# A two-layer decoder trunk on one core: accumulator tiles of one PSUM bank instead of two

## The chip, the core and the metric

One core of one Trainium2 chip runs the whole program in one launch. The metric is device time in microseconds (us) of that core. Before the change the runs took 1087.12, 1088.2 and 1092.54 us, so the median is 1088.2 us.

Engines are named as in the profile: PE is TensorE's matmul, PEld its weight load, DVE VectorE, ACT ScalarE, POOL GpSimd, SP SyncE, which here issues the weight DMAs. PSUM is the memory that matmuls write; the kernel allots it in banks of 128 partitions x 512 float32.

## The reference

Two layers over 256 positions of width 1024. Each layer is three residual steps on `x`:

```python
def swiglu(x, w_gate, w_up, w_down):
    return (jax.nn.silu(x @ w_gate) * (x @ w_up)) @ w_down
# per layer:
#   x = x + 0.5 * swiglu(rmsnorm(x, g0), ...)          first FFN, D_FF = 2816
#   x = x + concat(nsa_group(...), hgrn2(...)) @ w_out mix, fed by rmsnorm(x, g1) @ w_in
#   x = x + 0.5 * swiglu(rmsnorm(x, g2), ...)          second FFN
```

`nsa_group` is sparse attention (8 query heads, 2 key/value groups, compressed, selected and windowed keys, with norm and rotary on q and k), `hgrn2` is a gated linear recurrence with 4 heads. Everything is float32, and the weights of the two layers are read once.

## The kernel before

**The number format.** Each float32 weight tile is loaded by SP into a `raw` buffer (three of them, 512 KB each), rounded by ACT into `hi` (128x1024) and completed by DVE, or sometimes POOL, into `lo` = raw - hi. A ring of five hi/lo pairs feeds PE. Activations are split in the same way: `xx` holds the normalised, transposed input as high and low parts, `th`/`tl` the hidden layer of an FFN, `ah`/`al` the attention output. A product is three matmuls: hi x high, lo x high, hi x low.

**Two kinds of product.** `stream` (L462 and on, lines L486 to L488) keeps 128 positions of the activations stationary and moves 512 columns of weights; it runs once for each half `h` of the 256 positions. It serves the first FFN block, the `down` product and most of the mix. `wide_unit` (L501 and on) keeps 128 columns of weights stationary and moves all 256 positions. For the gate and up columns of the FFNs, paired blocks, it needs two matmuls: L519 moves the 512 columns "high | low" of `xx` against `hi`, L520 the 256 high ones against `lo`. Each block has 256 gate or up columns, that is two accumulators of one bank (index `c`), and an FFN has ten gate and ten up blocks. Lines L525 to L527 are the unpaired form in the mix.

**The accumulators.** PSUM has eight banks. `short` has three tiles and `po` one, for transposes and attention. The four others are two tiles, `acc0` and `acc1`, of two banks each; what the planner hands out as slots are the halves `t[:, i]` of these tiles. Gate blocks take both halves of `acc0`, up blocks both of `acc1`; a `stream` product of position half h takes one half of `acc{h}`.

**What follows a product.** Gate: ACT copies the right half of each bank into `sg` (both banks in one instruction, 128x512), DVE adds the left half, then the slots are released and ACT applies silu. Up: the same copy and add, then DVE multiplies with `sg`, ACT and DVE split the result into `th` and `tl`. In the mix, ACT and DVE read q, k, v and gates out of `acc` (names `buf`, `vv`, `xn`, `G`), and after each residual product DVE adds `acc` to `x` (L682).

**What sets the order.** The kernel is written as many small generators, which wait for keys (`wait`, `put`), take slots (`acq`, `rel`) and yield operations. The class `Sched` plans ahead of the run: it keeps an estimated end time for each engine and for each slot, gives each ready operation the time at which it could start plus a penalty (tables `PEN`, `STEP`, `PREP`, `FLOW`, `BIAS`, `SWITCH`, `FIRST`), and emits the smallest next. Each engine then runs its instructions in the emitted order. The waits between engines are not written by hand: they follow from which tile an instruction reads or writes, and `acc0` as a whole is one tile. Helpers record nearly all operations, so L335 is any ACT operation, L348 and L351 any two-operand one on DVE or POOL, L383 a transpose on PE.

Of the kernel before, what the change touches and what calls it, by code (L numbers as in the profile page):

```python
# [55 lines left out]

PEN = {"norm_turn": -0.1, "next_gain": 0.77, "gates_task": 0.15, "compress_task": -0.03, "level_task": 0.34, "boot":
       -1.1, "first_gain": -2.01, "first_norm": 0.02, "pad": 3.68, "hi_task": -0.6, "load_stream": 3.08, "done":
       -0.32, "kv_task": 1.05, "turn": -1.16, "load_w1": 2.22, "mix_prepare": 0.32, "c_turn": -1.52, "f_task": 0.04,
       "q_turn": 0.17, "kw_task": -4.22, "q_task": 0.59, "hg_task": 0.84, "hq_task": 0.54, "last_product": -0.25,  # L60
       "k_turn": 0.01, "products": -0.03, "turn_task": -0.1, "attend_task": 0.04, "out_task": 0.25, "k_task": 0.45,
       "cmp_task": -0.04, "first_turn": -0.43, "head_task": -0.08, "log_task": 0.04}
STEP = {'h': -0.47, 'g': 0.03, 'r': -0.0}
PREP = (-0.23, 0.26, 0.5, 0.92)
FLOW = (0.08, 0.28, 0.1)
BIAS = {'POOL': 0.14, 'ACT': -0.5}
SWITCH = 0.8

# [38 lines left out]
class Task:  # L107
    def __init__(self, gen, pen, deps, phase):
        self.gen, self.pen, self.deps, self.phase = gen, pen, list(deps), phase
        self.req = None  # L110

    def advance(self, value=None):
# [10 lines left out]
class Sched:  # L123
# [85 lines left out]
    def run(self):  # L209
        while self.tasks:  # L210
# [38 lines left out]
            self.free[eng] = issued if eng == "DMA" else end  # L249
            t.deps = [(end, eng)]  # L250
            self.advance(t, (end, eng))

# [50 lines left out]
class Trunk(Sched):  # L303
    def __init__(self, ctx, tc, io, out):
# [154 lines left out]
    def stream(self, h):  # L459
        for p, (a, b) in enumerate(self.phases):  # L460
            self.phase_at[h] = p
            for i in range(a, b):  # L462
# [27 lines left out]
                for t in range(2):  # L490
                    if i < BOOT:
                        yield wait(("lo", i, t))
                    yield self.P(3 * (WEIGHTS + k.n / 2400), lambda: mm(t))
                self.used[i] = self.used.get(i, 0) + 1
# [7 lines left out]
    def wide_unit(self, i, u, p):  # L502
# [35 lines left out]
        if u.last:  # L538
            self.spawn(k.done(k.ps[0]), phase=p, deps=self.keys[("wide", i)])
# [27 lines left out]
    def start(self):  # L567
        nc, per = self.nc, self.per
        self.X, self.XN, self.ss, self.rs = [], [], [], []
        self.XX = per.tile([128, 8, 2, 256], F32R, name="xx")  # L570
        self.XH, self.XL = self.XX[:, :, 0], self.XX[:, :, 1]
        for h in range(2):
# [6 lines left out]
        self.con = per.tile([128, C_END], F32, name="con")  # L579
        self.half = per.tile([128, 16], F32, name="half")  # L580
        self.grow, self.gcol = per.tile([8, 128], F32, name="grow"), per.tile([128, 8], F32, name="gcol")
# [139 lines left out]
    def ffn(self, l, pre):  # L721
# [27 lines left out]

        def both_parts(x, a):  # L750

            x, t = x.rearrange("p (c t) -> p c t", c=2), self.pair[a]
            yield self.A(x, t[:, :, 256:])
            yield self.tt(x, t[:, :, :256], x, OP.add)

        def wide_gate_done(b):
            def done(ps):
                yield wait(("open", p))
                (sg,) = yield acq("sg")
                yield from both_parts(sg, 0)  # L760
                yield rel("acc0", *ps)
                yield self.A(sg, sg, AF.Silu)
                st["wg", b] = sg
                yield put(("wg", p, b))
            return done

        def wide_up_done(b):
            def done(ps):
                (up,) = yield acq("sg")
                yield from both_parts(up, 1)  # L770
                yield rel("acc1", *ps)
                yield wait(("wg", p, b))
                sg = st["wg", b]
                yield self.tt(sg, up, sg, OP.mult)
                yield rel("sg", up)
                s = slice(2 + 2 * b, 4 + 2 * b)
                yield from self.split(st["th"][:, s], st["tl"][:, s], sg.rearrange("p (c t) -> p c t", c=2))
                yield rel("sg", sg)
                for h in range(2):
                    yield put(("h", p, h, 1 + b))  # L780
            return done
# [96 lines left out]
    def mix(self, l):  # L878
# [24 lines left out]
        def q_task(h, ps):  # L903
# [12 lines left out]
            for o, i in swap:  # L916
                a_.append((yield tt(t2[:, :, o], src[:, :, i], self.sg[:, h, 0:1, o].to_broadcast([128, H, 32]), OP.mult)))
            yield ("deps", a_)
            yield rel(f"acc{h}", ps)
# [648 lines left out]
```

## Time and profile before

| | before |
|---|---|
| runs | 1087.12, 1088.2, 1092.54 us |
| profiled execution | 1091.2 us, of which span 1089.4 us |
| PE busy | 1061.6 us, 97% of the span |
| DVE, ACT, POOL busy | 64%, 57%, 13% |
| DMA | 186 MB, mean 171 GB/s |

The profiled execution has 1.8 us around its span and is 3.0 us above the median of the runs. The stages of a layer follow each other: first FFN (to about 208 us in layer 0), mix (208 to 370 us), second FFN (to about 555 us); layer 1 repeats them. PE counts as busy from a matmul's start to a modelled end, so consecutive matmuls overlap in the record: the time that a matmul really takes from its neighbours is the distance from one start to the next.

### The profile page before, as it was taken

Reading aid. Unit: us, or ns where it says so; the run is one execution under the profiler, and the core shown is the slowest. Engines: PE = TensorE matmul, PEld = TensorE weight load, DVE = VectorE, ACT = ScalarE, POOL = GpSimd, SP = SyncE. Lnnn points to the kernel's source line nnn. Section 1 sums busy time; section 2 is a strip of 40 time slices with the busy share of each in tenths; the row PEclk is TensorE's granted clock in tenths of the full one; section 3 lists DMA queues with packets and bytes.
Section 4 is the critical chain, followed back from the end, with each engine's and each line's share of the span. In section 5 each row is a group of like instructions: output and inputs, shape, how many; then the busy total and the mean of one; then the engine's idle time right before and its main releaser. Section 6 shows DMA issues by size and latency. Waiting matters only on the chain.

```text
span 1089.4 us, 16298 instructions
## 1 busy us (share of the span) xinstructions
PE 1061.6 (97%) x6188; PEld 893.8 (82%) x6188; DVE 697.5 (64%) x1168; ACT 624.0 (57%) x1012; POOL 143.5 (13%) x111
## 2 busy tenths in 40 slices
PE   7999999999999999999999999999999989999998
PEld 4888888888787788888888888887978878888886
DVE  5776664668985666665366666448699666565633
ACT  6555554468884555564355555435789645555532
POOL 1000010211000012210031212002100001122110
PEclk9999999999999999999999999999999999999999
DMA  6766566556332566667566656656562326656653
GB/s 216 217 197 188 190 207 189 156 158 189 104 117 78 156 180 187 193 177 224 180 176 185 210 177 196 210 155 168 164 194 79 97 88 183 191 176 194 194 176 114
DMA packets 154159, 186.00 MB, mean 171 GB/s; under 512 B 7568, under 2 KB 117984, under 8 KB 154080
## 3 DMA queue, kind: packets, MB, share of 16 engines
q1 hardware_dynamic: 154080, 184.96, 56.5%
q8 instruction: 48, 0.79, 0.3%
q14 instruction: 31, 0.25, 0.1%
HBM read 183.89 MB, written 1.05 MB: 170 GB/s over the span
## 4 chain that ended last, share of the span: by engine, by line
PE 88%; DVE 5%; ACT 4%; issue 1%; DMA 1%; SPq 1%; POOL 0%; DVEq 0%; ACTq 0%; POOLq 0%
PE acc L519 27%; PE acc L520 14%; PE acc L486 12%; PE acc L487 12%; PE acc L488 12%; PE short L383 3%; PE po L1163 2%; ACT buf L335 1%; PE short L1381 1%; DVE lo L348 1%; PE acc L525 1%; PE acc L527 1%; PE acc L526 1%; ACT hi L335 1%; SPq L373 1%
## 5 line engine op out<-in xcount | busy, mean ns | idle before, releaser
L348 DVE TENSOR_TENSOR lo<-raw,hi 128x1024 fp32r<-128x1024 f32 (+2 forms) x300 | 356.4, 1202 | 177.0 <-ACT hi L335 176.6
L519 PE MATMUL acc<-xx,hi 128*128 128x512 f32 x1280 | 451.5, 397 | 0.0
L335 ACT ACTIVATE hi<-raw 128x1024 fp32r<-128x1024 f32 (+2 forms) x338 | 346.4, 1039 | 142.4 <-PE acc L488 83.2
L520 PE MATMUL acc<-xx,lo 128*128 128x256 f32 x1280 | 359.2, 281 | 0.0
L519 PEld LDWEIGHTS acc<-xx,hi 128*128 128x128 f32 x1280 | 240.3, 188 | 57.7
L520 PEld LDWEIGHTS acc<-xx,lo 128*128 128x128 f32 x1280 | 241.9, 189 | 0.2
L351 POOL TENSOR_TENSOR lo<-raw,hi 128x1024 fp32r<-128x1024 f32 x39 | 98.2, 2519 | 407.6 <-ACT hi L335 382.1
L486 PE MATMUL acc<-hi,th 128*128 128x512 f32 x352 | 140.0, 398 | 0.0
L488 PE MATMUL acc<-hi,tl 128*128 128x512 f32 x352 | 139.2, 396 | 0.0
L487 PE MATMUL acc<-lo,th 128*128 128x512 f32 x352 | 139.2, 395 | 0.0
L486 PE MATMUL acc<-hi,xx 128*128 128x512 f32 (+1 forms) x240 | 97.2, 405 | 8.0 <-DVE x L682 3.6
L348 DVE TENSOR_TENSOR sg<-acc,sg 128x512 f32<-128x512 f32 (+1 forms) x86 | 57.8, 672 | 54.9 <-ACT sg L335 54.7
L487 PE MATMUL acc<-lo,xx 128*128 128x512 f32 (+1 forms) x240 | 91.1, 380 | 0.2 <-DVE lo L348 0.2
L335 ACT ACTIVATE sg<-acc 128x512 f32<-128x512 f32 (+1 forms) x86 | 50.0, 581 | 71.3 <-PE acc L520 63.7
L488 PE MATMUL acc<-hi,xx 128*128 128x512 f32 (+1 forms) x240 | 90.8, 378 | 0.0
L488 PEld LDWEIGHTS acc<-hi,tl 128*128 128x128 f32 x352 | 66.2, 188 | 15.9
L486 PEld LDWEIGHTS acc<-hi,th 128*128 128x128 f32 x352 | 66.2, 188 | 15.7
L487 PEld LDWEIGHTS acc<-lo,th 128*128 128x128 f32 x352 | 66.2, 188 | 15.4
L335 ACT ACTIVATE th<-sg 128x512 fp32r<-128x512 f32 x40 | 25.3, 634 | 75.5 <-DVE sg L348 75.5
L486 PEld LDWEIGHTS acc<-hi,xx 128*128 128x128 f32 x240 | 45.1, 188 | 19.6 <-DVE x L682 5.3
L348 DVE TENSOR_TENSOR sg<-sg,sg 128x512 f32<-128x512 f32 x40 | 52.3, 1308 | 1.4
L488 PEld LDWEIGHTS acc<-hi,xx 128*128 128x128 f32 x240 | 45.1, 188 | 8.7
(211 smaller groups left out, 1149.8 us busy)
## 6 DMA issues: line engine op xcount, KB each, us to landing
raw<-in_ffn_w_down_dram SPq DMA_DIRECT2D x88, 512.0 KB, 4.3
raw<-in_ffn_w_gate_dram SPq DMA_DIRECT2D x80, 512.0 KB, 4.1
raw<-in_ffn_w_up_dram SPq DMA_DIRECT2D x80, 512.0 KB, 3.8
raw<-in_w_in_dram SPq DMA_DIRECT2D x48, 512.0 KB, 3.9
raw<-in_w_out_dram SPq DMA_DIRECT2D x16, 512.0 KB, 3.7
buf<-in_cmp_w_dram SPq DMA_DIRECT2D x16, 256.0 KB, 5.6
raw<-in_ffn_w_gate_dram SPq DMA_DIRECT2D x13, 256.0 KB, 2.8
raw<-in_ffn_w_up_dram SPq DMA_DIRECT2D x13, 256.0 KB, 3.1
```

The costliest lines, as they stand in the source:

```text
L335: return ("ACT", c, lambda: self.nc.scalar.activation(out, in_, func, **k), TABLES.get(func), False)
L348: alts = [("DVE", 0.065 + 0.00104 * n, lambda: self.nc.vector.tensor_tensor(out, a, b, op), None, not in_psum(a) and not in_psum(b))]
L351: alts.append(("POOL", 0.13 + 0.00213 * n, lambda: self.nc.gpsimd.tensor_tensor(out, a, b, op), None, True))
L373: return Op(("DMA", nbytes / 360e3, lambda: self.nc.sync.dma_start(out, in_), None, False))
L383: self.nc.tensor.transpose(o, i, self.ident[:i.shape[0], :i.shape[0]])
L486: f(ps[:, :k.n], ah, hi[:, t, :k.n], start=st, stop=False)
L487: f(ps[:, :k.n], ah, lo[:, t, :k.n], start=False, stop=False)
L488: f(ps[:, :k.n], al, hi[:, t, :k.n], start=False, stop=sp)
L519: f(self.pair[k.wide][:, c], hi[:, t, j], x, start=u.first and t == 0, stop=False)
L520: f(self.pair[k.wide][:, c, :256], lo[:, t, j], x[:, :256], start=False, stop=u.last and t == 3)
L525: f(ps[:, c], hi[:, t, j], xh, start=u.first and c == t == 0, stop=False)
L1163: nc.tensor.matmul(po[:, 64 * k:64 * k + 64], th[:, 128 * k:128 * k + 128], vv[:, vi, g], start=(i == k == 0), stop=False)
```

## The change

Four things are changed together.

1. The accumulators are four tiles of one bank, `acc00`, `acc01`, `acc10`, `acc11`, with two slots of `acc0` and two of `acc1` as before.
2. A gate or up block ends per bank: as soon as the matmuls of one index `c` of its last unit are emitted, its own evacuation starts, in operations of 128x256 instead of 128x512. The `sg` pool has eight tiles of 256 columns instead of five of 512. Key `("half", p, b)` makes the `down` product wait for both halves of a block.
3. `xx` is laid out with the two parts apart, [part, k, position] instead of [k, part, position]. For one k the high and low positions were 512 consecutive numbers of a partition; now they are two runs of 256, 8 KB apart, and the moving operand of L519 (L517 after) is that pair of runs.
4. The planner: a slot is free when the last operation of every engine of its task is over, not of the last operation alone; a 512-column product whose activations are not `xx` is priced 0.0065 us higher; the tables have new numbers. With these the emitted order changes.

```diff
-        self.pair = []
         for h in range(2):
-            t = psum.tile([128, 2, 512], F32, name=f"acc{h}")
-            self.pair.append(t)
-            self.slots[f"acc{h}"] = [(t[:, i], []) for i in range(2)]
+            self.slots[f"acc{h}"] = [(bank(f"acc{h}{i}"), []) for i in range(2)]
...
-            x = self.XX[:, u.kt + t].rearrange("p a t -> p (a t)")
-            f(self.pair[k.wide][:, c], hi[:, t, j], x, start=u.first and t == 0, stop=False)
-            f(self.pair[k.wide][:, c, :256], lo[:, t, j], x[:, :256], start=False, stop=u.last and t == 3)
+            f(ps[c].rearrange("p (a t) -> p a t", a=2), hi[:, t, j], self.XX[:, :, u.kt + t], start=u.first and t == 0, stop=False)
+            f(ps[c][:, :256], lo[:, t, j], self.XH[:, u.kt + t], start=False, stop=u.last and t == 3)
...
-                yield self.P(0.707 if k.paired else 6 * (WEIGHTS + 256 / 2400), lambda: two(c, t))
+                done = yield self.P(0.707 if k.paired else 6 * (WEIGHTS + 256 / 2400), lambda: two(c, t))
+            if k.paired and u.last:
+                self.spawn(k.done(c, k.ps[0][c]), phase=p, deps=[done])
...
-        self.XX = per.tile([128, 8, 2, 256], F32R, name="xx")
-        self.XH, self.XL = self.XX[:, :, 0], self.XX[:, :, 1]
+        self.XX = per.tile([128, 2, 8, 256], F32R, name="xx")
+        self.XH, self.XL = self.XX[:, 0], self.XX[:, 1]
...
-        def both_parts(x, a):
+        def both_parts(x, ps):
-            x, t = x.rearrange("p (c t) -> p c t", c=2), self.pair[a]
-            yield self.A(x, t[:, :, 256:])
-            yield self.tt(x, t[:, :, :256], x, OP.add)
+            yield self.A(x, ps[:, 256:])
+            yield self.tt(x, ps[:, :256], x, OP.add)
...
-                self.slots[arg].append((x, list(t.deps)))
+                self.slots[arg].append((x, list(t.deps) + [d for d in t.last.values() if d not in t.deps]))
...
-            self.slots["sg"] = [(pool.tile([128, 512], F32, name=f"sg{i}"), []) for i in range(5)]
+            self.slots["sg"] = [(pool.tile([128, 256], F32, name=f"sg{i}"), []) for i in range(8)]
...
-FIRST = (-0.31, -0.01, 0.65, 0.74, 1.09, 0.54, -1.08, 0.72)
+FIRST = (-0.15, -0.01, 0.61, 0.68, 1.4, 0.59, -1.31, 0.93)
```

The orders below show what this moves. The number behind a name tells tiles apart; a wait is shown with the engine whose work is waited for. In the changed kernel the three lines of `stream` are L485 to L487, the transposes L382, ACT's helper L334.

PE before, early in the mix of layer 0, where the products of q and k/v for the second half of the positions both stand in tile `acc1`:

```order
L486 MATMUL acc1_64<-hi0_72,xx_82 128x512
L487 MATMUL acc1_64<-lo0_73,xx_82 128x512
L488 MATMUL acc1_64<-hi0_72,xx_82 128x512
L486 MATMUL acc1_64<-hi0_72,xx_82 128x512 [waits Activation_49]
L487 MATMUL acc1_64<-lo0_73,xx_82 128x512
L488 MATMUL acc1_64<-hi0_72,xx_82 128x512
L486 MATMUL acc0_63<-hi1_74,xx_82 128x512 [waits DVE_49]
```

And PE after at the same place, with q in `acc11` and k/v in `acc10`:

```order
L485 MATMUL acc11_66<-hi3_80,xx_84 128x512
L486 MATMUL acc11_66<-lo3_81,xx_84 128x512
L487 MATMUL acc11_66<-hi3_80,xx_84 128x512
L485 MATMUL acc10_65<-hi0_74,xx_84 128x512
L486 MATMUL acc10_65<-lo0_75,xx_84 128x512
L487 MATMUL acc10_65<-hi0_74,xx_84 128x512
L485 MATMUL acc10_65<-hi0_74,xx_84 128x512
L486 MATMUL acc10_65<-lo0_75,xx_84 128x512
L487 MATMUL acc10_65<-hi0_74,xx_84 128x512
L485 MATMUL acc00_63<-hi1_76,xx_84 128x512 [waits Activation_49]
```

The wait for ACT between the two groups on `acc1` is gone; the one that is left after is on the ring's `hi1`. The order of the products themselves is the same.

PE before, at the end of the mix in layer 0, where the output product's second column block follows the first in tile `acc1`:

```order
L486 MATMUL acc1_64<-hi3_78,xx_82 128x512
L487 MATMUL acc1_64<-lo3_79,xx_82 128x512
L488 MATMUL acc1_64<-hi3_78,xx_82 128x512
L486 MATMUL acc1_64<-hi0_72,xx_82 128x512 [waits DVE_49]
L487 MATMUL acc1_64<-lo0_73,xx_82 128x512
L488 MATMUL acc1_64<-hi0_72,xx_82 128x512
L383 MATMUL short2_67<-ident_91,xn0_84 128x128 x4
L486 MATMUL acc1_64<-hi0_72,xx_82 128x512
```

And PE after at the same place:

```order
L485 MATMUL acc10_65<-hi3_80,xx_84 128x512
L486 MATMUL acc10_65<-lo3_81,xx_84 128x512
L487 MATMUL acc10_65<-hi3_80,xx_84 128x512
L485 MATMUL acc11_66<-hi0_74,xx_84 128x512
L486 MATMUL acc11_66<-lo0_75,xx_84 128x512
L487 MATMUL acc11_66<-hi0_74,xx_84 128x512
L382 MATMUL short2_69<-ident_93,xn0_86 128x128 [waits DVE_49]
L382 MATMUL short2_69<-ident_93,xn0_86 128x128 x3
L485 MATMUL acc11_66<-hi0_74,xx_84 128x512
```

The wait for DVE ahead of the second block is gone; a wait for DVE now stands ahead of the transposes of `xn0`, three matmuls later.

ACT before, in the first FFN of layer 0, around one gate and one up block:

```order
L335 ACTIVATE sg3_122<-acc1_64 128x512 [waits PE_49]
L335 ACTIVATE hi0_72<-raw2_71 128x1024 [waits DMAHW0_49,Activation_49]
L335 ACTIVATE th_124<-sg1_120 128x512 [waits DVE_49]
L335 ACTIVATE hi1_74<-raw0_69 128x1024 [waits DMAHW1_49,PE_49,Activation_49]
L335 ACTIVATE sg2_121<-acc0_63 128x512 [waits PE_49]
L335 ACTIVATE sg2_121<-sg2_121 128x512 [waits DVE_49]
```

And ACT after:

```order
L334 ACTIVATE sg0_121<-acc11_66 128x256 [waits PE_49]
L334 ACTIVATE hi3_80<-raw2_73 128x1024 [waits DMAHW2_49,Activation_49]
L334 ACTIVATE th_129<-sg6_127 128x256 [waits DVE_49]
L334 ACTIVATE sg2_123<-acc10_65 128x256 [waits PE_49]
L334 ACTIVATE th_129<-sg7_128 128x256 [waits DVE_49]
L334 ACTIVATE hi0_74<-raw0_71 128x1024 [waits DMAHW3_49,Pool_49]
L334 ACTIVATE sg4_125<-acc01_64 128x256 [waits PE_49]
L334 ACTIVATE sg4_125<-sg4_125 128x256 [waits DVE_49]
L334 ACTIVATE sg5_126<-acc00_63 128x256 [waits PE_49]
L334 ACTIVATE sg5_126<-sg5_126 128x256 [waits DVE_49]
```

Each operation on 512 columns has become two on 256. In the whole program 160 such operations of ACT and 160 of DVE become 320 each, and POOL takes 9 of the `lo` operations instead of 39; the 30 others stand on DVE.

## Rows read from the trace of the kernel before

**Rows 1.** Page, part 4: the chain that ended last, shares by engine

```profile
PE 88%; DVE 5%; ACT 4%; issue 1%; DMA 1%; SPq 1%; POOL 0%; DVEq 0%; ACTq 0%; POOLq 0%
```

**Rows 2.** Windows by stage: stretch, length, busy us (instructions) by engine, clock, DMA

```profile
26.00:145.00 119.00, 119.00 (x673) 102.70 (x672) 81.02 (x94) 68.65 (x88) 0.00 (x0) 1.00 0.64 197
208.00:370.00 162.00, 154.32 (x1161) 130.68 (x1160) 125.87 (x340) 115.19 (x254) 15.26 (x22) 1.00 0.46 132
370.00:490.00 120.00, 119.89 (x673) 103.42 (x672) 77.42 (x77) 66.00 (x85) 21.90 (x10) 1.00 0.64 188
742.00:904.00 162.00, 154.06 (x1159) 130.42 (x1158) 125.52 (x340) 115.93 (x254) 15.11 (x21) 1.00 0.45 131
```

**Rows 3.** Waits of PE: line, waited for, us in total, times, longest

```profile
PE acc L486 <- DVE x L682: 3.6, 4, 1.0
...
PE acc L486 <- ACT buf L335: 2.1, 4, 0.7
PE acc L486 <- ACT G L335: 1.4, 2, 0.7
...
PE acc L486 <- ACT xn L335: 1.1, 2, 0.7
PE acc L486 <- DVE buf L348: 1.0, 2, 0.5
```

**Rows 4.** Timeline of PE at 219 us: start, duration, instruction, idle before

```profile
219.34 0.39 PE L488 MATMUL acc<-hi,xx 128*128 128x512 f32 x1
220.42 0.50 PE L486 MATMUL acc<-hi,xx 128*128 128x512 f32 x1 [0.69 <-ACT buf L335]
220.76 0.39 PE L487 MATMUL acc<-lo,xx 128*128 128x512 f32 x1
```

**Rows 5.** Timeline of ACT at the same time

```profile
219.77 0.60 ACT L335 ACTIVATE buf<-acc 128x512 f32<-128x512 f32 x1 [0.70 <-PE acc L488]
```

**Rows 6.** Chain from 330 to 372 us: start, duration, piece

```profile
341.65 1.03 POOL ost L377
...
343.45 0.49 PE po L1432 x2
...
359.91 0.69 DVE x L682
360.65 0.50 PE acc L486
```

**Rows 7.** Window in the middle of layer 0's mix, columns as in rows 2

```profile
280.00:300.00 20.00, 19.81 (x213) 16.41 (x212) 18.60 (x85) 18.44 (x64) 1.06 (x2) 1.00 0.28 80
```

**Rows 8.** Instructions by form, ACT and DVE: count, busy us, mean ns, idle before

```profile
L335 ACT ACTIVATE sg<-acc 128x512 f32<-128x512 f32 x80 | 47.7, 596 | 64.2 <-PE acc L520 63.7
...
L335 ACT ACTIVATE sg<-acc 128x256 f32<-128x256 f32 x6 | 2.3, 386 | 7.1 <-PE acc L488 7.1
...
L348 DVE TENSOR_TENSOR lo<-raw,hi 128x1024 fp32r<-128x1024 f32 x286 | 346.3, 1225 | 171.3 <-ACT hi L335 171.0
L348 DVE TENSOR_TENSOR sg<-acc,sg 128x512 f32<-128x512 f32 x80 | 55.3, 691 | 53.3 <-ACT sg L335 53.0
...
L348 DVE TENSOR_TENSOR sg<-acc,sg 128x256 f32<-128x256 f32 x6 | 2.5, 419 | 1.7 <-ACT sg L335 1.7
```

**Rows 9.** Page, part 5: the two matmuls of a gate or up pair

```profile
L519 PE MATMUL acc<-xx,hi 128*128 128x512 f32 x1280 | 451.5, 397 | 0.0
...
L520 PE MATMUL acc<-xx,lo 128*128 128x256 f32 x1280 | 359.2, 281 | 0.0
```

**Rows 10.** Windows of line L519 alone, second FFN of layer 0, first of layer 1

```profile
400.00:480.00 80.00, 80.00 (x228) 42.59 (x227) 1.00 0.64 190
580.00:660.00 80.00, 80.00 (x232) 43.13 (x231) 1.00 0.64 190
```

**Rows 11.** Chain at 215 us: products with `xx` stationary, columns as in rows 6

```profile
214.97 0.23 PE acc L486
...
218.15 0.23 PE acc L488
```

More of the change, by code (lines that the diff above doesn't have):

```diff
@@ L55 @@
 ORDER = ('q', 'kv', 'kw', 'hf', 'hq', 'hi', 'hg')
[L57 to L62, printed above, removed]
+PEN = {"norm_turn": -0.1, "next_gain": 0.34, "gates_task": 0.15, "compress_task": -0.03, "level_task": 0.35, "boot":
+       -1.55, "first_gain": -3.16, "first_norm": 0.01, "pad": 4.23, "hi_task": -0.74, "load_stream": 3.09, "done":
+       -0.32, "kv_task": 1.24, "turn": -3.97, "load_w1": 2.22, "mix_prepare": 0.46, "c_turn": -0.45, "f_task": 0.13,
+       "q_turn": 0.17, "kw_task": -2.2, "q_task": 0.55, "hg_task": 0.78, "hq_task": 0.52, "last_product": -0.25,
+       "k_turn": 0.01, "products": -0.03, "turn_task": -0.1, "attend_task": 0.04, "out_task": 0.27, "k_task": 0.45,
+       "cmp_task": -0.01, "first_turn": -0.44, "head_task": -0.08, "log_task": 0.1}
 STEP = {'h': -0.47, 'g': 0.03, 'r': -0.0}
[L64 to L67, printed above, removed]
+PREP = (-0.22, 0.28, 0.5, 0.92)
+FLOW = (0.11, 0.29, 0.54)
+BIAS = {'POOL': 0.13, 'ACT': -0.5}
+SWITCH = 0.79
 def constants():
@@ L110, in __init__ @@
         self.req = None
+        self.last = {}
     def advance(self, value=None):
@@ L249, in run @@
             self.free[eng] = issued if eng == "DMA" else end
-            t.deps = [(end, eng)]
-            self.advance(t, (end, eng))
+            token = (end, eng)
+            t.deps, t.last[eng] = [token], token
+            self.advance(t, token)
 def four(t):
@@ L492, in stream @@
                         yield wait(("lo", i, t))
-                    yield self.P(3 * (WEIGHTS + k.n / 2400), lambda: mm(t))
+                    yield self.P(3 * (WEIGHTS + k.n / 2400 + 0.0065 * (k.n == 512 and u.act != self.xact)), lambda: mm(t))
                 self.used[i] = self.used.get(i, 0) + 1
@@ L534, in wide_unit @@
             for t in (0, 2):
-                yield self.P(0.707 if k.paired else 6 * (WEIGHTS + 256 / 2400), lambda: two(c, t))
+                done = yield self.P(0.707 if k.paired else 6 * (WEIGHTS + 256 / 2400), lambda: two(c, t))
+            if k.paired and u.last:
+                self.spawn(k.done(c, k.ps[0][c]), phase=p, deps=[done])
         yield rel("ring", self.split_w.pop(i))
         yield put(("wide", i))
-        if u.last:
+        if u.last and not k.paired:
             self.spawn(k.done(k.ps[0]), phase=p, deps=self.keys[("wide", i)])
@@ L579, in start @@
         self.con = per.tile([128, C_END], F32, name="con")
-        self.half = per.tile([128, 16], F32, name="half")
+        self.half = per.tile([128, 8], F32, name="half")
         self.grow, self.gcol = per.tile([8, 128], F32, name="grow"), per.tile([128, 8], F32, name="gcol")
@@ L748, in both_done, with done @@
             yield rel("short", pt)
-        def both_parts(x, a):
-            x, t = x.rearrange("p (c t) -> p c t", c=2), self.pair[a]
-            yield self.A(x, t[:, :, 256:])
-            yield self.tt(x, t[:, :, :256], x, OP.add)
+        def both_parts(x, ps):
+            yield self.A(x, ps[:, 256:])
+            yield self.tt(x, ps[:, :256], x, OP.add)
         def wide_gate_done(b):
-            def done(ps):
+            def done(c, ps):
                 yield wait(("open", p))
                 (sg,) = yield acq("sg")
-                yield from both_parts(sg, 0)
-                yield rel("acc0", *ps)
+                yield from both_parts(sg, ps)
+                yield rel("acc0", ps)
                 yield self.A(sg, sg, AF.Silu)
-                st["wg", b] = sg
-                yield put(("wg", p, b))
+                st["wg", b, c] = sg
+                yield put(("wg", p, b, c))
             return done
         def wide_up_done(b):
-            def done(ps):
+            def done(c, ps):
                 (up,) = yield acq("sg")
[L770 to L773, printed above, removed]
+                yield from both_parts(up, ps)
+                yield rel("acc1", ps)
+                yield wait(("wg", p, b, c))
+                sg = st["wg", b, c]
                 yield self.tt(sg, up, sg, OP.mult)
                 yield rel("sg", up)
-                s = slice(2 + 2 * b, 4 + 2 * b)
-                yield from self.split(st["th"][:, s], st["tl"][:, s], sg.rearrange("p (c t) -> p c t", c=2))
+                s = 2 + 2 * b + c
+                yield from self.split(st["th"][:, s], st["tl"][:, s], sg)
                 yield rel("sg", sg)
-                for h in range(2):
-                    yield put(("h", p, h, 1 + b))
+                if ("half", p, b) in self.keys:
+                    yield wait(("half", p, b))
+                    for h in range(2):
+                        yield put(("h", p, h, 1 + b))
+                else:
+                    yield put(("half", p, b))
             return done
```

2 lines of the change are left out of this document (1 added, 1 removed).

## The prediction, made before the changed kernel ran

> **What bounds the kernel now.** I read the chain of waits first. PE holds 88% of it, DVE and ACT together 9% [rows 1]: the time is the matmuls, plus what PE waits for. The windows by stage say where it waits. In an FFN PE is busy for all of a stretch, 119.00 of 119 us, while DVE is busy for 81.02 and ACT for 68.65 [rows 2]; in the mix of layer 0 PE is busy 154.32 of 162 us, so 7.7 us idle, and layer 1's mix is taken as the same. What is to be gained without fewer matmuls lies in those idle times. The list of PE's waits names them [rows 3]. Five of its lines have one thing in common, found by following each wait in the order back to the two addresses: the matmul that waits writes one bank of `acc0` or `acc1`, and the ACT or DVE operation waited for reads the other bank of the same tile. No data pass between them. The timeline shows one such case: ACT reads `acc` from 219.77 to 220.37 [rows 5], and PE starts its next matmul at 220.42 although the last one began at 219.34 [rows 4]. These five lines sum to 3.6 + 2.1 + 1.4 + 1.1 + 1.0 = 9.2 us in 14 waits.
>
> **Part 1, one-bank tiles.** It removes these waits wholly: in the order before each is there, in the order after no matmul on an accumulator waits for a reader of another bank. What one costs is more than the idle time shown, since busy time has a modelled end. With `xx` stationary a matmul takes 227 ns from start to start (214.97 to 218.15 us are 14 of them) [rows 11]. The case shown lost 220.42 - 219.34 - 0.23 = 0.85 us, 0.16 more than the 0.69 printed, and the first matmul after it took 220.76 - 220.42 = 0.34 instead of 0.23 us, 0.11 more [rows 4]. So 14 x 0.27 = 3.8 us on top of 9.2, 13.0 us in all.
>
> How much of it stays? The waits for `x` and `G` (5.0 us, 6 waits, so 6.6 us with the additions) stand at the end of the mix and lead into the FFN, where PE never waits; this part stays. One doubt is the output norm before it, ACT to DVE to POOL `ost` to PE `po` at 341.65 to 343.45 us [rows 6]: the few steps ahead of it go through a ring buffer that PE frees, so it comes earlier with PE. The waits for `buf` and `xn` (4.2 us, 8 waits, 6.4 us) stand early in the mix. Behind them PE runs into a stretch where DVE is busy 18.60 and ACT 18.44 of 20 us [rows 7]; if these two set the pace, PE arrives earlier and waits there. I keep half, 3.2 us. Sum: 6.6 + 3.2 = 9.8 us, with 6.6 and 13.0 as ends.
>
> **Part 2, evacuation per bank.** 160 operations of ACT on 512 columns become 320 on 256: 2 x 386 - 596 = 176 ns more each, 28 us; on DVE 2 x 419 - 691 = 147 ns, 24 us [rows 8], the accumulator reads standing for the silu, multiply and split of the same size. 30 `lo` operations move from POOL to DVE, at 1.225 us each [rows 8] 37 us. Over four FFNs that is 7 us on ACT and 15 on DVE for each. In the window 26 to 145 us they had 50 and 38 us idle [rows 2], so PE's own matmuls hide all of it, and I cost it at nothing. If the cover were gone, as in a stretch where DVE runs at 93%, up to 61 us could show; no accumulator is evacuated by these operations there. The gain of starting one bank's evacuation 4 pairs earlier is nothing either, since no FFN window has PE idle by over 0.11 us [rows 2]. The Trainium skill ("Advanced Engine Details and Errata", section The Read-Write Bubble) speaks against this part: ACT and DVE pay a latency between instructions, so tiles should be large, of 512 or 1024 elements. Its mechanism is in the trace, as the 176 and 147 ns above; taken as a verdict on the time it would give 1078 + 52, and the row of 119.00 busy us of 119 says that it doesn't reach PE.
>
> **Part 3, the layout of `xx`.** The stationary loads of `xx` stay contiguous. The 512-column matmul of 1280 pairs [rows 9] now reads two runs. Nothing before does that. A pair with one run takes 80 / 228 = 351 ns in one FFN and 80 / 232 = 345 ns in another with the same shapes [rows 10], so there is a spread of 6 ns that the shapes don't explain. From below, all four FFNs could run at 345: the three slower have 960 pairs, x 6 = -5.8 us. From above, two runs could cost what two separate matmuls of 256 do: such a one takes 351 - 227 = 124 ns here [rows 10, 11], two 248, so 21 ns more, x 1280 = +27 us. I take nothing, nearer to the lower end, since a matmul's time goes by its columns (124 ns for 256, 227 for 512), whose number stays, and the spread of 6 ns is the only effect of place that the rows have.
>
> **Part 4, the order.** The sequence of products is the same at the places shown; DVE's and ACT's operations are shuffled in the mix. The mixes' idle time that isn't false is 2 x 7.7 - 9.2 = 6.2 us [rows 2, 3]: a better order could win some of it, a worse one double it. I take nothing, with 6 us as ends.
>
> Sum: the profiled execution took 1091.2 us (span 1089.4, 1.8 around it); 1091.2 - 9.8 = 1081.4. It was 3.0 us above the median of the runs, which I take as its own scatter: 1078.
>
> **The rivals.**
>
> *The pace of DVE and ACT takes it back.* For it: 93% and 92% busy in the middle of the mix [rows 7]. If all the early part is lost and the new order loses 2 us, 1088.2 - 6.6 + 2 = 1084. Against it: that stretch has PE busy 19.81 of 20 us too, so PE is hardly waiting there.
>
> *The pairs run at the quicker pace everywhere.* 1078 - 5.8 = 1072. For it: one FFN does so already with identical instructions [rows 10], so it hangs on something that shifts with placement or timing, which this change touches. Against it: nothing says in which direction.
>
> *The change doesn't do what it says.* The false waits were covers: behind each, PE would wait for something else, as the ring or the next transposed input (after, a wait for DVE stands three matmuls behind the second place shown). Then the time stays, 1088. Against it: at 360.65 PE starts as soon as DVE's addition to `x` is over, 359.91 + 0.69 [rows 6], so that wait alone held it, and all 14 would have to be replaced.
>
> *Slower: the two runs of `xx` cost a start.* One mechanism, at L517 after: the moving operand's second run begins 8 KB away, and each of the 1280 matmuls pays for it. The bounds above are 0 and 21 ns; half, 11 ns, gives +14 us: 1092. It decides from 9.8 us / 1280 = 8 ns on, where the kernel is no faster, and from 12 ns it is slower by more than 0.5%. For it: a start that PE can't overlap costs 0.11 us after a wait [rows 4]. Against it: no row has such a cost within an instruction. The Trainium skill ("SBUF — State Buffer", its note on SBUF cachelines) puts the cost of strides on lines of 16 bytes: reads that stay in a line run at full speed. Two runs of 1 KB each cross one line more, so by it this rival costs nothing; no run here shows it.
>
> **How the numbers follow.** Forecast 1078 with its own range of 1074 to 1083: 0.50. Taken back, 1084: 0.15. Quicker pairs, 1072: 0.12. Nothing, 1088: 0.13. Two runs, 1092 and up: 0.10. About 0.5%, 5.4 us, is what can be told from no change, so faster means under 1082.8 and slower over 1093.6. Faster: 0.47 of the forecast, 0.12 of the quicker pairs, 0.06 of the second case, 0.65. Slower: 0.05 of the two runs and 0.04 for an order that loses its 6 us on top of the case of nothing, 0.09. Same: the rest, 0.26. The range of 1069 to 1089 leaves out about 0.1 above and less than 0.1 below.
>
> **What would show it.** Right: the five lines of PE's waits are gone, or shrink to waits under 0.2 us; PE idles about 10 us less in the two mixes; the FFN windows have PE busy throughout, with DVE at about 96 us and ACT at 76 of a stretch like 26 to 145; L517 keeps 227 to 233 instructions in 80 us. Wrong in part 3: fewer than 222 of them. Wrong in part 1: new waits of PE `acc` lines on ACT or DVE in the mix, of the same size, or longer waits of `short` and `po` between 264 and 320 us. Wrong in part 2: PE waits for `sg`, `th` or `lo` inside an FFN.

## The result: 9 us faster, and the profile after

The changed kernel takes 1079.8 us in the median (1078.70 to 1080.61), against 1088.98 for the kernel before in the same runs: a ratio of 0.9911, 95% interval 0.9883 to 0.9939. The forecast was 1078, from a gain of 9.8 us. The profiled execution took 1078.7 us, its span 1076.8, which is 12.6 less than the span before. One later execution of the changed kernel took 1474.03 us at a granted clock of 0.654; no time or ratio below counts it.

PE's waits in the changed kernel, in the columns of [rows 3], the whole list:

```profile
PE short L382 <- DMA grow<-in_ffn_norm_dram: 3.2, 1, 3.2
PE short L382 <- DVE xgl L651: 3.0, 1, 3.0
PE short L382 <- DMA x<-in_x_dram: 2.0, 2, 1.3
PE short L382 <- DVE ad L1390: 1.8, 2, 1.2
PE short L1198 <- DVE mx L1202: 0.9, 4, 0.3
PE short L1384 <- DVE hx L347: 0.7, 2, 0.4
PE short L1401 <- ACT vcb L334: 0.6, 2, 0.3
PE short L382 <- DVE xn L697: 0.6, 1, 0.6
PE short L382 <- DVE kk L347: 0.5, 2, 0.2
PE short L1199 <- DVE kl L347: 0.3, 2, 0.2
PE acc L486 <- DVE lo L347: 0.2, 1, 0.2
```

All five lines of [rows 3] are gone; the only product on an accumulator that still waits does so for a weight. The first three lines are the start of the program. New is the wait for `ad`, 1.8 us.

Windows of the same stretches as [rows 2], after, with layer 1's mix:

```profile
26.00:145.00 119.00, 119.00 (x673) 102.87 (x672) 82.81 (x129) 72.57 (x128) 2.59 (x1) 1.00 0.61 187
208.00:370.00 162.00, 158.64 (x1190) 135.39 (x1189) 130.03 (x350) 116.91 (x256) 17.35 (x22) 1.00 0.48 140
370.00:490.00 120.00, 120.00 (x671) 103.63 (x670) 82.03 (x125) 72.87 (x125) 0.00 (x0) 1.00 0.60 185
742.00:904.00 162.00, 159.35 (x1195) 136.84 (x1195) 129.53 (x345) 118.39 (x257) 16.64 (x21) 1.00 0.48 140
```

PE fills the FFN windows as before although DVE and ACT have more to do there, and the windows of the mixes have 3.4 and 2.7 us of idle PE instead of 7.7 and 7.9.

The operations of part 2, after, in the columns of [rows 8]:

```profile
L347 DVE TENSOR_TENSOR sg<-acc,sg 128x256 f32<-128x256 f32 x166 | 69.9, 421 | 43.8 <-ACT sg L334 43.7
L334 ACT ACTIVATE sg<-acc 128x256 f32<-128x256 f32 x166 | 63.0, 379 | 83.2 <-PE acc L518 73.8 <-PE acc L487 8.2
L347 DVE TENSOR_TENSOR sg<-sg,sg 128x256 f32<-128x256 f32 x80 | 34.6, 433 | 2.7
```

The first two cost about what the few such rows before had said, 421 and 379 ns against 419 and 386; the third is the multiply, which before was this row:

```profile
L348 DVE TENSOR_TENSOR sg<-sg,sg 128x512 f32<-128x512 f32 x40 | 52.3, 1308 | 1.4
```

For where the time went I measured the stages from start to start of PE's matmuls in the traces: "pairs" from the first to the last L519 of an FFN (L517 or L516 in the other kernels), "mix" from the last matmul of the first FFN's `down` product to the first pair of the second FFN. Each column is one profiled execution; the last two are experiments told below. The rows of pairs differ in part by the pace of the pairs, told at the end of the experiments.

| us | before | changed | part 1 alone | part 1 alone, again |
|---|---|---|---|---|
| to the first pair | 27.30 | 27.19 | 27.50 | 27.52 |
| pairs, FFN 1 and 2 | 114.82, 117.14 | 116.22, 117.10 | 114.82, 117.14 | 112.78, 115.11 |
| pairs, FFN 3 and 4 | 115.21, 117.14 | 117.10, 115.04 | 115.16, 117.14 | 115.19, 115.05 |
| mix, layer 0 and 1 | 166.97, 167.29 | 161.08, 159.28 | 159.47, 159.31 | 159.24, 159.50 |
| span | 1089.4 | 1076.8 | 1074.1 | 1068.0 |

The gain is in the mixes, 5.9 + 8.0 = 13.9 us. The `down` stretches are equal within 0.3 us in all of them.

### The profile page after: what moved, and what is told of

It is laid out like the page before. It is cut to its first block, busy times and chain, and to the rows that moved or that the text cites. A ratio compares the mean times of both kernels' runs of the same rounds, so it can differ in the third digit from the quotient of the medians.

```text
span 1076.8 us, 16674 instructions
## 1 busy us (share of the span) xinstructions
PE 1057.7 (98%) x6188; PEld 893.0 (83%) x6188; DVE 722.5 (67%) x1361; ACT 647.7 (60%) x1169; POOL 73.6 (7%) x81
## 4 chain that ended last, share of the span: by engine, by line
PE 87%; DVE 5%; ACT 3%; DMA 2%; SPq 1%; issue 1%; POOL 0%; DVEq 0%; ACTq 0%; POOLq 0%
PE acc L517 28%; PE acc L518 14%; PE acc L485 12%; PE acc L486 12%; PE acc L487 12%; PE short L382 3%; PE po L1166 2%; DMA raw<-in_w_in_dram 1%; DVE lo L347 1%; PE short L1384 1%; DVE SP L347 1%; ACT hi L334 1%; SPq L372 1%; DVE buf L1202 1%; DVE buf L347 1%
## 5 line engine op out<-in xcount | busy, mean ns | idle before, releaser
L347 DVE TENSOR_TENSOR lo<-raw,hi 128x1024 fp32r<-128x1024 f32 (+2 forms) x330 | 391.2, 1203 | 165.3 <-ACT hi L334 163.1
L517 PE MATMUL acc<-xx,hi 128*128 128x512 f32 x1280 | 451.5, 398 | 0.0
L334 ACT ACTIVATE hi<-raw 128x1024 fp32r<-128x1024 f32 (+2 forms) x338 | 347.7, 1038 | 134.8 <-DMA raw<-in_ffn_w_down_dram 53.7
L517 PEld LDWEIGHTS acc<-xx,hi 128*128 128x128 f32 x1280 | 240.4, 188 | 58.6
L485 PE MATMUL acc<-hi,th 128*128 128x512 f32 x352 | 139.9, 398 | 0.0
L487 PE MATMUL acc<-hi,tl 128*128 128x512 f32 x352 | 139.2, 395 | 0.0
L334 ACT ACTIVATE sg<-acc 128x256 f32<-128x256 f32 x166 | 63.0, 379 | 83.2 <-PE acc L518 73.8
L347 DVE TENSOR_TENSOR sg<-acc,sg 128x256 f32<-128x256 f32 x166 | 69.9, 421 | 43.8 <-ACT sg L334 43.7
L485 PE MATMUL acc<-hi,xx 128*128 128x512 f32 (+1 forms) x240 | 94.3, 393 | 0.0
L487 PE MATMUL acc<-hi,xx 128*128 128x512 f32 (+1 forms) x240 | 90.8, 379 | 0.0
L487 PEld LDWEIGHTS acc<-hi,tl 128*128 128x128 f32 x352 | 66.1, 188 | 16.0
L485 PEld LDWEIGHTS acc<-hi,th 128*128 128x128 f32 x352 | 66.2, 188 | 15.6
L486 PEld LDWEIGHTS acc<-lo,th 128*128 128x128 f32 x352 | 66.2, 188 | 15.5
L350 POOL TENSOR_TENSOR lo<-raw,hi 128x1024 fp32r<-128x1024 f32 x9 | 23.2, 2577 | 608.0 <-ACT hi L334 454.3
L334 ACT ACTIVATE sg<-sg 128x256 f32<-128x256 f32 x80 | 33.5, 418 | 47.7 <-DVE sg L347 47.7
L334 ACT ACTIVATE th<-sg 128x256 fp32r<-128x256 f32 x80 | 33.5, 418 | 44.6 <-DVE sg L347 43.9
L347 DVE TENSOR_TENSOR tl<-sg,th 128x256 fp32r<-128x256 f32 x80 | 34.0, 425 | 36.3 <-ACT th L334 36.1
L487 PEld LDWEIGHTS acc<-hi,xx 128*128 128x128 f32 x240 | 45.0, 188 | 8.3
```

The source lines that it names most:

```text
L334: return ("ACT", c, lambda: self.nc.scalar.activation(out, in_, func, **k), TABLES.get(func), False)
L347: alts = [("DVE", 0.065 + 0.00104 * n, lambda: self.nc.vector.tensor_tensor(out, a, b, op), None, not in_psum(a) and not in_psum(b))]
L350: alts.append(("POOL", 0.13 + 0.00213 * n, lambda: self.nc.gpsimd.tensor_tensor(out, a, b, op), None, True))
L485: f(ps[:, :k.n], ah, hi[:, t, :k.n], start=st, stop=False)
L486: f(ps[:, :k.n], ah, lo[:, t, :k.n], start=False, stop=False)
L487: f(ps[:, :k.n], al, hi[:, t, :k.n], start=False, stop=sp)
```

## The experiments

Ratios are to the kernel before run on the same chip in turn, with 95% intervals.

**Part 1 alone, and part 1 undone.** The first kernel has the old order, layout and tables:

```diff
-            t = psum.tile([128, 2, 512], F32, name=f"acc{h}")
-            self.slots[f"acc{h}"] = [(t[:, i], []) for i in range(2)]
+            self.slots[f"acc{h}"] = [(bank(f"acc{h}{i}"), []) for i in range(2)]
...
-            yield self.A(x, t[:, :, 256:])
+            yield Op(("ACT", 0.052 + 0.000833 * 512, lambda: [self.nc.scalar.activation(x[:, c], t[:, 256:], AF.Copy) for c, t in enumerate(a)], None, False))
...
```

> Part 1 alone: the kernel before with four accumulator tiles of one bank. Its order of operations, its layout of xx and its tables are those of before; the copy and the addition that empty gate and up blocks, which can't span two tiles, are two instructions of 256 columns each, issued back to back, everything else stays at 512. Theory of the prediction: the 14 waits of PE on a reader of the other bank go (13.0 us), the late ones (6.6 us) are kept in full, the early ones by half: 9.8 us less than before, about 1079, a ratio of 0.991. Rival, DVE and ACT take the early part back: 6.6 us less, 1082, ratio 0.994. Rival, nothing is taken back: 13 us less, 1076, ratio 0.988. Rival, the gain comes from the order or the layout and not from the tiles: no change, 1089.

Measured 1075.1 us, 0.9857 (0.9841 to 0.9873), and in a second set 1075.8, 0.9865 (0.9842 to 0.9889): the case in which nothing is taken back, and a little beyond it. PE runs the same 6188 instructions in the same order as before, so each start can be set against its partner. The 1061st is 0.24 us later than before, the 1081st 1.35 us earlier, the 1201st 2.84; from there to the 1921st, through the whole stretch in which DVE and ACT are busiest, the lead stays between 2.63 and 2.84 us, but for 42 instructions around 265 us with up to 3.51, and at the 1921st it is 2.70. After the mix it is 7.29. In layer 1 it goes from 7.33 to 10.71 by the end of the busy stretch, and to 15.31 by the end of the mix, which it keeps to the end of the program.

The other way round the changed kernel got its two-bank tiles back, the same edit reversed.

> The changed kernel with part 1 undone: acc0 and acc1 are tiles of two banks again, handed out as halves; order, layout and evacuation by 256 columns are those of the changed kernel. Theory: the false waits come back in the mix, 10 to 13 us, about 1090 to 1093; in the FFNs ACT's and DVE's reads of one bank must now wait for PE's matmuls into the other, which PE doesn't feel as long as the next block writes the other tile. Rival, the gain lies in the order: it stays at 1080. Rival, the evacuation per bank needs the split tiles: PE waits inside the FFNs too, and the time is over 1100.

Measured 1219.8 us, 1.1186 (1.1169 to 1.1204). The rival of the last sentence was right, and far beyond its 1100. PE's waits, first lines:

```profile
PE acc L518 <- DVE sg L348: 46.7, 79, 0.7
PE acc L518 <- ACT sg L335: 36.0, 76, 0.5
PE acc L486 <- ACT buf L335: 5.6, 10, 0.7
PE acc L486 <- DVE x L683: 3.6, 4, 1.0
```

And the timeline within one gate or up block of this kernel, all engines (start, duration, instruction, idle before):

```profile
97.84 0.28 PE L519 MATMUL acc<-xx,lo 128*128 128x256 f32 x1
98.15 0.38 ACT L335 ACTIVATE sg<-acc 128x256 f32<-128x256 f32 x1 [0.99 <-PE acc L519]
98.44 1.05 ACT L335 ACTIVATE hi<-raw 128x1024 fp32r<-128x1024 f32 x1
98.59 0.50 PE L518 MATMUL acc<-xx,hi 128*128 128x512 f32 x1 [0.47 <-ACT sg L335]
```

The evacuation of the first bank starts while PE still has the second bank of the same block to fill; with one tile for both PE stops after the first, at 97.84, until ACT has copied it (0.47 us idle), and once more for DVE (the first line of its waits). The pairs of the four FFNs take 590.7 us instead of 465.5. In this order part 2 costs about 140 us without part 1.

**Part 1 for acc1 alone.**

```diff
-            self.slots[f"acc{h}"] = [(bank(f"acc{h}{i}"), []) for i in range(2)]
+            t = None if h else psum.tile([128, 2, 512], F32, name="acc0")
+            self.slots[f"acc{h}"] = [(bank(f"acc{h}{i}") if h else t[:, i], []) for i in range(2)]
```

> Part 1 for acc1 only: acc1 is two tiles of one bank, acc0 is one of two banks as before; the rest as in the kernel with part 1 alone. By the trace of before, the waits of PE on the other bank of acc1 sum to 3.2 us a layer, with about 0.1 us each for the slower first matmul 3.6: 7.2 us less than before, about 1082. It asks about the wait of PE's po matmul for kk (1.15 us of idle time in each mix), which went with part 1 although it is none of PE's waits on a bank. Theory: before, ACT's second copy of G out of acc0 waited for PE's matmuls into the other bank of acc0, and everything behind it on ACT came late; then this wait of po is still there, with the waits on acc0. Rival, it only went because PE was late in the mix for the sum of the waits ahead: then it is gone or small here too, and the time is about 1080 or less.

Measured 1081.2 us, 0.9926 (0.9906 to 0.9947), 8.1 us less than before. The expectation's theory named the wrong tile: with the waits on `acc0` still there, the wait of `po` is gone. Before, it was this line of PE's waits (columns as in [rows 3]):

```profile
PE po L1432 <- DVE kk L348: 2.3, 2, 1.1
```

Of the two operations of ACT on G, the first belongs to the first half of the positions and reads `acc0`, the second to the second half and reads `acc1`, so splitting `acc1` frees the second. ACT before, around the two (timeline, columns as in [rows 5]):

```profile
333.71 1.28 ACT L335 ACT_TABLE_LOAD   x1
335.41 0.60 ACT L335 ACTIVATE G<-acc 128x512 f32<-128x512 f32 x1 [0.42 <-PE acc L488]
337.76 0.60 ACT L335 ACTIVATE G<-acc 128x512 f32<-128x512 f32 x1 [1.76 <-PE acc L488]
```

ACT with only `acc1` split:

```profile
333.92 1.09 ACT L333 ACTIVATE G<-acc 128x512 f32<-128x512 f32 x2 [0.43 <-PE acc L486]
335.04 1.06 ACT L333 ACTIVATE hi<-raw 128x1024 fp32r<-128x1024 f32 x1
```

Before, the second operation on G waited 1.76 us for a product of another bank (1.75 in layer 1), and `hi`, `lo`, `ost` and `kk` came behind it. The chain before, columns as in [rows 6], which has its end:

```profile
338.39 1.07 ACT hi L335
339.48 1.23 DVE lo L348
340.70 0.61 DVE ost L1438
...
342.70 0.70 DVE kk L348
```

With only `acc1` split the second runs right behind the first, although PE's own wait for the first is still there, and this `hi` starts 3.35 us earlier where PE is 1.49 us earlier. PE's waits on `acc0` in this kernel:

```profile
PE acc L484 <- ACT xn L333: 1.8, 2, 1.2
PE acc L484 <- DVE x L680: 1.6, 2, 0.8
...
PE acc L484 <- ACT G L333: 1.4, 2, 0.7
```

They also show a gain given back: the wait for the copy of V (`xn`) grew from 1.1 [rows 3] to 1.8 us, since PE reaches it earlier and the copy hasn't moved as much (in layer 0 the copy is 2.17 us earlier, and PE's wait 0.64 us instead of 0.40).

**The layout of xx.**

```diff
-            f(ps[c].rearrange("p (a t) -> p a t", a=2), hi[:, t, j], self.XX[:, :, u.kt + t], ...
+            f(ps[c], hi[:, t, j], self.XX[:, u.kt + t].rearrange("p a t -> p (a t)"), ...
...
```

> The changed kernel with part 3 undone: xx is laid out as before, so that the moving operand of the paired 512-column matmul is one run of 512 numbers instead of two of 256. Nothing else changes. Theory: the two runs cost nothing, 1080, with 228 to 232 of these matmuls in 80 us as before. Rival, the two runs cost 3 to 21 ns on each of 1280: 4 to 27 us less than the changed kernel. Rival, the layout moved the pairs to the quicker pace of 345 ns: up to 6 us more.

Measured 1078.0 us, 0.9884 (0.9869 to 0.9898), inside the interval of the changed kernel (and 1077.6 us for that kernel in a later set, below), with pairs at 347 and 353 ns in both layouts: two runs cost nothing that can be seen here.

**The tables.** Only the numbers were put back.

```diff
-FIRST = (-0.15, -0.01, 0.61, 0.68, 1.4, 0.59, -1.31, 0.93)
+FIRST = (-0.31, -0.01, 0.65, 0.74, 1.09, 0.54, -1.08, 0.72)
...
```

> The changed kernel with the old numbers in the planner's tables; tiles, layout, evacuation and the planner's new rules stay. Theory: the new numbers are worth little, 1080, within the 6 us of idle time in the mixes that the order could win or lose. Rival, the new order carries the gain: 1086 or more. Where it differs, the difference stands in PE's waits in the mix and not in the FFNs.

Measured 1081.9 us, 0.9926 (0.9910 to 0.9941). The mixes take 160.54 and 159.99 us, as long as the changed kernel's. What differs is the start, where no theory had looked: the first pair comes at 34.76 us instead of 27.19. PE idles 4.54 us and soon after 1.63 us for `xgl` of DVE, and from 20.00 to 33.50 us its granted clock is 0.50, the level of 1.2 GHz, at which a 512-column matmul takes 0.43 us from start to start instead of 0.23; the changed kernel has one such wait, of 3.02 us, and a clock of 0.79 from 20 to 25 us and of 1.00 behind. How much of the 7.57 us each of these makes is not measured. The pairs of this execution ran at 347 ns in all four FFNs, which gave 6.6 us of it back.

**Part 2 doubled, and part 2 undone.** First, two copies and two additions of 128 columns instead of one of 256, each two planned as one operation:

```diff
-            yield self.A(x, ps[:, 256:])
-            yield self.tt(x, ps[:, :256], x, OP.add)
+            yield Op(("ACT", 0.052 + 0.000833 * 256, lambda: [self.nc.scalar.activation(x[:, s:s + 128], ps[:, 256 + s:384 + s], AF.Copy) for s in (0, 128)], None, False))
+            yield self.V(256, lambda: [self.nc.vector.tensor_tensor(x[:, s:s + 128], ps[:, s:s + 128], x[:, s:s + 128], OP.add) for s in (0, 128)])
```

> The changed kernel with the suspected cost of part 2 doubled: the copy on ACT and the addition on DVE that empty an accumulator of a gate or up block are two instructions of 128 columns each instead of one of 256, 160 more on each engine, the order otherwise unchanged. By the prediction's reckoning (one 128-column read of acc takes 276 ns against 386, so about 166 ns more for each pair) this is about 27 us more of ACT and as much of DVE. Theory: the matmuls of the FFNs hide it, no change against the changed kernel run beside it, 0 to 1 us. Rival, the evacuation stands on the path: 5 us more or up to 27.

> The changed kernel as it is, on the same chip as the runs beside it, as the reference for them: about 1080 by its first runs, a ratio of 0.991, and 4 to 5 us above the kernel with part 1 alone (0.986).

Measured 1080.7 us, 0.9917 (0.9898 to 0.9935), against 1077.6 us, 0.9894 (0.9872 to 0.9916), for the changed kernel beside it: the intervals overlap, but the 3.0 us between the medians are more than the theory's 1. The traces decide for the FFNs. The two spans are 3.1 us apart; the first pair comes 1.25 us later with the doubled evacuation, and its second FFN, mostly at the slower pace of the pairs (below), takes 117.83 us against 115.61. The window from 904 us, first with the doubled evacuation, then of the changed kernel in its first profile, columns as in [rows 2]:

```profile
904.00:1020.00 116.00, 116.00 (x651) 100.33 (x651) 81.49 (x163) 72.37 (x163) 0.00 (x0) 1.00 0.59 184
```

```profile
904.00:1020.00 116.00, 116.00 (x659) 100.84 (x658) 80.19 (x123) 71.79 (x123) 0.00 (x0) 1.00 0.60 187
```

DVE and ACT have 40 instructions more each and PE is busy throughout in both; the 651 and 659 matmuls are the two paces (below). In the third and fourth FFN, where this kernel and the changed one beside it both ran at the slower pace, the pairs took 117.08 us in each. One thing does reach PE, in the second FFN: there it waits for a `lo` of DVE, 0.3 us in the changed kernel beside it (0.54 us from start to start) and 0.5 us with the doubled evacuation (0.73, and 0.2 at an earlier block). The kernel with one run of `xx` has it too, with 0.2 us. The first profile of the changed kernel has no such wait among its pairs, nor have the profiles of the kernels that evacuate whole blocks.

Then part 2 undone, with parts 1, 3 and 4 kept, blocks evacuated as a whole as in the kernel with part 1 alone:

```diff
-                self.spawn(k.done(c, k.ps[0][c]), phase=p, deps=[done])
...
-        if u.last and not k.paired:
+        if u.last:
             self.spawn(k.done(k.ps[0]), phase=p, deps=self.keys[("wide", i)])
...
-            self.slots["sg"] = [(pool.tile([128, 256], F32, name=f"sg{i}"), []) for i in range(8)]
+            self.slots["sg"] = [(pool.tile([128, 512], F32, name=f"sg{i}"), []) for i in range(5)]
```

> The changed kernel with part 2 undone: gate and up blocks end as a whole, with five sg tiles of 512 columns and silu, multiply and split at 512, as in the kernel with part 1 alone; the layout of xx, the planner's new rules and its new numbers are those of the changed kernel. Theory A, the evacuation per bank takes back what the changed kernel lacks against part 1 alone: about 1075. Theory B, the new order takes it back (the changed kernel's mix of layer 0 is 1.6 us longer and its first pairs start with more waits): 1079 to 1081. Theory C, neither: the difference is the pace of the pairs, which comes out by chance in each FFN at 347 or 353 ns; then the mixes and the starts are as long as with part 1 alone and the number of FFNs at the slower pace decides, 2.1 us each.

Measured 1076.5 us, 0.9877 (0.9857 to 0.9898). Its mixes are 159.34 and 159.31 us, as with part 1 alone; its pairs in FFN 1, with 116.67, are as slow as the changed kernel's (116.22). So the 1.6 us in layer 0's mix go with part 2, and the 1.4 us in FFN 1 with part 4 (with part 3 undone the two were still there, 161.02 and 116.22). No gate or up block is evacuated in the mix, so what part 2 costs there comes presumably from the order that the planner makes of it; no run shows this alone. Both are within the intervals of the times; only the traces tell them apart.

**The pace of the pairs.** Two theories on what sets it both fell. The edits, to the kernel with part 1 alone, repeat a block's first matmul, for nothing. In the first kernel it is repeated in every block, with 512 columns in gate blocks and 256 in up blocks:

```diff
+            if u.first and c == t == 0:
+                n = 256 if k.wide else 512
+                f(ps[c][:, :n], hi[:, t, j], x[:, :n], start=True, stop=True)
             f(ps[c], hi[:, t, j], x, start=u.first and t == 0, stop=False)
```

In the two that follow it is repeated in the first up block of three FFNs only, with 256 columns and with 512.

> The kernel with part 1 alone, with a disturbance at the start of each of the 80 paired blocks: the block's first matmul is issued twice, the first time for nothing (all 512 columns in gate blocks, 256 in up blocks), which adds about 0.23 or 0.12 us a block, 14 us in all. It asks what sets the pace of the pairs, which stays at 347 or 353 ns for a whole FFN. If the pace is a phase that is caught when a run of pairs starts and then kept, blocks of one FFN will now show both paces. If it belongs to the FFN (its place in memory, what DVE and ACT do there), all blocks of an FFN keep the pace that it has with part 1 alone: 353, 353, 347, 353.

> Part 1 alone, and in the three FFNs whose pairs run at 353 ns (the first, second and fourth) the first matmul of the first up block is issued once more with 256 columns, for nothing; three instructions more in all. Theory of the phase: in the kernel with a repeat in every block a repeat of 256 columns turned the pace over each time and one of 512 left it; so these three FFNs go to 347 from their second block on, 304 of 320 pairs, 3 x 304 x 6.67 ns = 6.1 us less, and the repeats cost 3 x 0.12: 5.7 us less than the kernel beside it, about 1069.5. Rival, the turn was by chance: paces mixed, within 2 us of it. Rival, the pace returns to 353 within the FFN: no gain.

> The same three places, but the repeated matmul has all 512 columns. Theory of the phase: no turn, the paces stay at 353, 353, 347, 353 and the repeats cost 3 x 0.23 = 0.7 us more than the kernel beside it. Rival, any additional instruction turns the pace: about 1070, as with 256 columns.

> The kernel with part 1 alone as it is, as the reference for the runs beside it: 1075 by its first runs, a ratio of 0.986, with the pace of the pairs at 353, 353, 347, 353 ns in the four FFNs.

With a repeat in every block (1088.65 us, one run) the mean distance of the pairs does change inside an FFN, in strict order: 347, 353, 353, 347, 347, 353, 353 and so on by blocks. So the pace is not fixed for an FFN. From that I expected that a repeat of 256 columns turns the pace, and I had read it the wrong way round: in this trace the pace turns at each of the 36 repeats of 512 columns that stand within an FFN (as at 41.62 us, from 347 to 353), and stays at those of 256. Nor does either do it alone: with 256 the three FFNs had 353, 347 and 347 ns before and behind the repeat (1074.1 us, 0.9857, 0.9838 to 0.9876), with 512 in the same places the same paces (1075.0 us, 0.9863, 0.9839 to 0.9887); neither differs from the kernel beside it (0.9865). And that kernel, the very program of the first experiment, had other paces in this execution. Line L516, its 512-column matmul of a pair, in the first FFN and the last:

```profile
60.00:140.00 80.00, 80.00 (x232) 43.17 (x231) 1.00 0.65 197
...
920.00:1000.00 80.00, 80.00 (x232) 43.20 (x231) 1.00 0.63 191
```

All four FFNs ran at 347 ns, and this is the fastest run of the study, 1069.73 us, while its sisters took 1073.5 to 1078.4. The kernel with only `acc1` split had all four at 353 in its profiled execution, 1084.26 us, among sisters of 1079 to 1085. So the pace goes with the execution and the FFN in it, not with the kernel; what sets it stays open.

## Why the prediction was right, and where its sum was off

**Part 1, that the waits go:** right; none of the five lines is left, and with one-bank tiles alone the time falls by more than the whole change brings.

**Part 1, the size of 13.0 us:** too small. The mixes with part 1 alone are 7.5 and 8.0 us shorter, 15.5. The sum had counted only PE's own waits for readers of an accumulator. The same tiles also made ACT wait for PE: the second operation on G, 1.76 us, whose delay came back to PE through `ost` as the wait of `po` for `kk`. That is 1.3 us from start to start in each mix, 2.6 in all, and just what was missing: the late part of the two layers gained 4.59 and 4.60 us by the starts, 9.2 in all, where the sum had 6.6. The forecast had passed over that wait, as something that goes with a ring buffer; the chain shows that it stood behind G on ACT.

**Part 1, that half of the early part is lost:** wrong. With the order unchanged nearly all of it was kept: at the end of the busy stretch the two layers have gained 2.94 and 3.38 us, 6.3 of the 6.4. DVE and ACT at 93% [rows 7] were not the pace. Before, ACT's 1.56 us of idle time in that window all ended with work of PE, and of DVE's 1.40 us 0.62 did, the rest nearly all with work of ACT; with part 1 both come earlier, as PE does. The busy share alone didn't show this; that PE was busy for 19.81 of the same 20 us did, and the prediction had it as the argument against.

**Part 2, hidden in the FFNs:** right but for about half a us, by the FFN windows and by the doubled evacuation. The prediction's own sign against it, PE waiting for a `lo` inside an FFN, did come in one FFN of the changed kernel's second profile, with 0.3 us. ACT's 72.57 us in the window to 145 us is near the 76 expected; DVE's 82.81 is far under 96, for two reasons: the multiply, 1308 ns at 512 columns in the profile before, takes 433 at 256, so two are 866; and POOL had no `lo` to give away in this window, 0.00 us before [rows 2]. The latency between instructions of the Trainium skill ("Advanced Engine Details and Errata", The Read-Write Bubble) is in these rows, 2 x 379 - 596 = 162 ns for each copy cut in two, and stayed off the path but for that wait. What the prediction didn't see is that in this order part 2 needs part 1, by 140 us.

**Part 3, nothing:** right. One count in it is off without effect: two runs of 1 KB fill as many lines of 16 bytes as one of 2 KB, 128, and not one more.

**Part 4, nothing, within 6 us:** right in size, but the new order and the evacuation that it plans took back about 3 us of part 1's gain by the stages: 1.6 in layer 0's mix and 1.4 in the first FFN. Its pieces are larger than their sum: with the old numbers in the tables the start is 7.57 us longer, in a kernel that has everything else of the change.

So the mechanism was right, and that the size came out too is in part luck: two errors in one direction, 2.6 us not counted and 3.2 us wrongly taken off, made the gain too small, and the other parts cost about 3 us where the forecast had said nothing. The 12.6 us between the spans and the 9.2 between the medians differ by the scatter of the executions: the one profiled before is 2.2 us above its median, the one after 1.1 below. One source of scatter is the pace, which is worth 320 x 6.67 ns = 2.1 us in one FFN. **The quicker pairs:** both paces occur in the kernel before and in the changed one, with one quick FFN of four in the profile before and in each of the two profiles after; no run shows that the change touches it. **Nothing, and slower by two runs:** excluded by the part-1 kernel and by the layout.

The best of these kernels is the one with part 1 alone, at 1075 to 1076 us (0.9857 and 0.9865), though its interval touches that of the changed kernel.

## What to carry to other kernels

A tile that is larger than what its users touch makes waits in both directions: sum the waits of the producer for the readers, but look also for readers that wait for the producer, and follow what is queued behind them. Before an early evacuation of half a block, make sure that the two halves are not one tile. And a busy share of 93% on the helpers doesn't say that they set the pace: where the engine on the path was hardly idle, a gain ahead of that stretch was carried through it here.

## What the runs showed of the chip that was not expected

A pair of matmuls with 512 and 256 columns takes 346.7 or 353.3 ns from start to start at a granted clock of 1.00 in both cases, and in most profiles it holds one of the two through an FFN of 320 pairs. It can turn inside one. In the second FFN of the kernel with one run of `xx` it turned from 347 to 353 at 466.67 us, where one distance was 390 ns, and back at 478.01 us, where PE waited for a `lo` (a distance of 811 ns). The same wait in the changed kernel, with 885 ns, left it at 347. Runs of one kernel scatter by up to 8.6 us (1069.73 to 1078.38), about the four steps of 2.1 us that four FFNs allow; that the pace makes all of this scatter is not shown.
